# Layer-0 attention: the reciprocals of the softmax sums go through scratch memory by DMA, not through TensorE transposes

## The chip, the cores and the metric

The kernel runs on one core of a Trainium2 chip. The metric is the device time of one execution, in microseconds (us); a smaller time is better. The engines are TensorE (PE; its weight loads are listed as PEld), VectorE (DVE), ScalarE (ACT), GpSimd (POOL) and SyncE (SP), and SP's queue issues nearly all DMAs.

## What is computed

Four layers of a diffusion trunk on 512 latent tokens and 256 context tokens of width 1024: grouped-query attention, neighbourhood attention, a convolution module and a Fourier mixer, each followed by an MLP. The change is in layer 0, whose mixer is this (16 query heads, 4 key heads, head size 64; `ctx_out` is true there, so the context's own attention is computed too):

```python
def gqa_attend(q, k, v):
    s = jnp.einsum('bqkgd,bnkd->bkgqn', q, k, preferred_element_type=jnp.float32)
    p = jax.nn.softmax(s, axis=-1).astype(v.dtype)
    return jnp.einsum('bkgqn,bnkd->bqkgd', p, v)
...
    ob = lax.map(lambda q: gqa_attend(q, k_all, v_all), qb)
    yl = ob.transpose(1, 0, 2, 3, 4, 5).reshape(B, S, AT_WIDTH) @ w_o
...
        oc = gqa_attend(qc.reshape(B, C, AT_KV_HEADS, AT_GROUP, HEAD_DIM), kc, vc)
        yc = oc.reshape(B, C, AT_WIDTH) @ w_o
```

The softmax's division is not made on the probabilities. The kernel multiplies exp(s) with the values first, and the product with 1/sum afterwards.

## The kernel before

Layer 0's attention is `l0b`. Its work is 8 pairs of heads (`pair`) x 3 parts of 256 query tokens (`part`: 0 and 1 are latent tokens with all 768 keys, 2 is the context with its 256 keys) x 2 heads (`hh`). A group is one (pair, part), so there are 24 groups. Below, (p,1) is part 1 of pair p.

For each item, `front` runs twice (`u`), for 128 tokens each time. It makes the scores (L612, PE into `ps_s`), their negated maximum (L614, DVE), the exponentials `p` with their sums in `sums` (L616, ACT), transposes of `p` (L621, PE into `ps_st`), and the split of these into a high and a low part `pt` (L104 on ACT, L105 on DVE). `back`, one item later, multiplies with the values (L635, PE into `ps_pv`, which is one buffer).

When both heads of a group are through, `recip_rows` turns the sums round. Sums lie with tokens on partitions, and the product lies with tokens along the free axis. The reciprocal is taken on DVE (L555), spread to 64 columns a head on DVE (L557, `tmp_q`), transposed twice on PE (L559, into a `ps_st` buffer, of which there are three) and copied out by ACT (L561, `tmp_r`, called `rb` in the code). `fold` adds the two halves of the product (L567 on ACT, L568 on DVE, twice each a group, into `tmp_t`). `scale_pv` multiplies `tmp_t` with `rb` on POOL (L573), and splits the result into `o` (the cast L104 on ACT, the subtraction L105 on POOL).

SP's queue in this stage holds the stores of the last `qd` rows (L530), a load of 768 KB of `q` for each pair (L586), six loads of output weights (`raw`, L113), and at the end `sb`, the four loads of `x` (L667) and the `araw` tiles for the projection with `wo0` that follows.

The order on each engine's queue is not the code's. A scheduler sets it at build time by its own estimates (L1338), and the engines then run their queues strictly in that order: an instruction that waits holds all that stand behind it on its engine.

Of the kernel before, what the change touches and what calls it, by code (L numbers as in the profile page):

```python
# [9 lines left out]
F = mybir.dt.float32  # L10
# [6 lines left out]
P = 128  # L17
# [7 lines left out]
HD = 64  # L25
# [24 lines left out]
class Trunk:  # L50
# [499 lines left out]
    def recip_rows(self, sums, w, wk, rp):  # L550
# [10 lines left out]
        nc.scalar.copy(out=rb, in_=rp[:, :w])  # L561
        return rb

    def fold(self, pv, hh, t):

        a, b = slice(hh * HD, hh * HD + HD), slice(HD - hh * HD, 2 * HD - hh * HD)
        self.nc.scalar.copy(out=t[a], in_=pv[b])  # L567
        self.nc.vector.tensor_tensor(out=t[a], in0=pv[a], in1=t[a], op=ALU.add)  # L568
# [7 lines left out]
    def l0b(self):  # L576
        nc, io = self.nc, self.io
# [3 lines left out]
        wk = self.open("att0", "right")  # L581
# [7 lines left out]
        def keys(part):  # L589
            return (0, 6) if part < 2 else (4, 2)  # L590
# [34 lines left out]
        def back(pair, part, hh, half):  # L625

            k0, nk = keys(part)
            if hh == half == 0:
                pvs[pair, part] = self.ps("pv")
            sums, pv = groups[pair, part], pvs[pair, part]  # L630
            pt = heads[pair, part, hh]
            o_ = pv[:, hh * 256:hh * 256 + 256]
            for c in range(k0 + half * nk // 2, k0 + (half + 1) * nk // 2):
                for s in range(2):
                    nc.tensor.matmul(o_, self.vp[:, c, pair // 2].rearrange("p s d -> p (s d)"), pt[s][:, :, c - k0],  # L635
                                     start=(hh == s == 0 and c == k0), stop=(hh == s == 1 and c == 5))
            if hh == half == 1:
                t0 = part * 256
                rb = self.recip_rows(sums, 256, wk, self.ps("st"))
                t = self.tmp("t", 256)  # L640
                for e in range(2):
                    self.fold(pv[:, e * 256:e * 256 + 256], e, t)
                self.scale_pv(t, rb, (o[pair][:, 0, t0:t0 + 256], o[pair][:, 1, t0:t0 + 256]))
# [4 lines left out]
        for i in range(len(work) + 1):  # L648
            if i < len(work) and work[i][1:] == (0, 0) and work[i][0] < 7:
                load(work[i][0] + 1)  # L650
            for u in range(2):
                if i < len(work):
                    front(*work[i], u)
                if i > 0:
                    back(*work[i - 1], u)
            if i == LATE:
                self.late()
                self.open("att0b", "right")
# [699 lines left out]
```

## Time and profile before

| what | us |
|---|---|
| median of 3 runs | 2750.66 |
| lowest and highest run | 2748.48 and 2753.79 |
| the profiled execution, its own time | 2748.76 |
| its span in the trace | 2747.0 |
| layer-0 attention, from the first reciprocal to the last fold | 191.8 to 386.4 |
| one pair of heads in the steady part of it | 23.7 |

The profile is of one execution. A row gives busy time and idle time of instructions, and the idle time is put down to the instruction that came last. In the layer-0 attention three engines are busy at once, so a share of busy time alone does not name the one that sets the pace; waits between them must be read with it.

### The profile page before, as it was taken

Reading aid. Unit: us, or ns where it says so; the run is one execution under the profiler, and the core shown is the slowest. Engines: PE = TensorE matmul, PEld = TensorE weight load, DVE = VectorE, ACT = ScalarE, POOL = GpSimd, SP = SyncE. Lnnn points to the kernel's source line nnn. Section 1 sums busy time; section 2 is a strip of 40 time slices with the busy share of each in tenths; the row PEclk is TensorE's granted clock in tenths of the full one; section 3 lists DMA queues with packets and bytes.
Section 4 is the critical chain, followed back from the end, with each engine's and each line's share of the span. In section 5 each row is a group of like instructions: output and inputs, shape, how many; then the busy total and the mean of one; then the engine's idle time right before and its main releaser. Section 6 shows DMA issues by size and latency. Waiting matters only on the chain.

```text
span 2747.0 us, 39895 instructions
## 1 busy us (share of the span) xinstructions
PE 2638.0 (96%) x15472; PEld 2316.5 (84%) x15472; DVE 1776.1 (65%) x2827; ACT 1154.8 (42%) x2052; POOL 405.4 (15%) x359
## 2 busy tenths in 40 slices
PE   7989899999999999998999999998999998999998
PEld 5878778888888888988988889888888887988888
DVE  7988879766453372268766657998666657644445
ACT  3458864212121342268523335656322245533323
POOL 2321212000000030034200004543000012200002
PEclk8999999999999999999999999999999999999999
DMA  7431234445442256488466644213466633333334
GB/s 269 133 123 36 77 120 147 139 145 153 137 140 85 77 168 209 138 201 190 161 206 207 190 147 139 77 47 107 133 212 200 206 124 107 123 115 94 98 100 123
DMA packets 124844, 384.85 MB, mean 140 GB/s; under 512 B 17264, under 2 KB 37872, under 8 KB 123632
## 3 DMA queue, kind: packets, MB, share of 16 engines
q1 hardware_dynamic: 121392, 379.17, 44.2%
q10 hardware_dynamic: 3264, 3.15, 0.3%
q8 instruction: 122, 2.00, 0.3%
q14 instruction: 66, 0.54, 0.1%
HBM read 354.98 MB, written 27.26 MB: 139 GB/s over the span
## 4 chain that ended last, share of the span: by engine, by line
PE 49%; DVE 4%; DMA 2%; ACT 1%; issue 0%; POOL 0%; DVEq 0%; SPq 0%; ACTq 0%; POOLq 0%
PE ps_mm L124 15%; PE ps_mm L125 15%; PE ps_mm L127 15%; DVE ps_st L1162 1%; DMA k<-k 1%; DMA q<-q 1%; PE ps_cv L124 1%; PE ps_cv L125 1%; PE ps_cv L127 1%; DVE h L182 0%; PE ps_s L881 0%; PE ps_pt L890 0%; PE ps_cv L995 0%; PE ps_cv L998 0%; PE ps_cv L999 0%
## 5 line engine op out<-in xcount | busy, mean ns | idle before, releaser
L104 ACT CAST wh<-raw 128x1024 fp32r<-128x1024 f32 (+1 forms) x397 | 419.6, 1060 | 1030.6 <-PE ps_mm L125 606.5
L105 DVE TENSOR_TENSOR wl<-raw,wh 128x1024 fp32r<-128x1024 f32 (+1 forms) x368 | 463.7, 1262 | 372.6 <-ACT wh L104 369.5
L194 POOL TENSOR_TENSOR S<-S,tmp_q 128x256 f32<-128x256 f32 (+1 forms) x104 | 144.8, 1392 | 1684.8 <-ACT tmp_q L193 1680.7
L124 PE MATMUL ps_mm<-u,wh 128*128 128x512 f32 (+1 forms) x1088 | 374.9, 346 | 0.0
L125 PE MATMUL ps_mm<-u,wh 128*128 128x512 f32 (+1 forms) x1088 | 373.8, 345 | 0.0
L127 PE MATMUL ps_mm<-u,wl 128*128 128x512 f32 (+1 forms) x1088 | 373.6, 346 | 0.0
L125 PE MATMUL ps_mm<-hm,wh 128*128 128x512 f32 (+1 forms) x912 | 331.2, 365 | 0.0
L127 PE MATMUL ps_mm<-hm,wl 128*128 128x512 f32 (+1 forms) x912 | 331.0, 365 | 0.0
L124 PE MATMUL ps_mm<-hm,wh 128*128 128x512 f32 (+1 forms) x912 | 328.2, 366 | 1.1 <-ACT hm L181 1.1
L223 DVE CUSTOM_DVE_ANT_0 prod<-araw,sb 128x1024 bf16<-128x1024 f32 x224 | 276.4, 1234 | 6.5 <-DMA araw<-in_ada 5.3
L206 DVE SCALAR_TENSOR_TENSOR x<-ps_mm,mod,x 128x256 f32<-128x256 f32 (+1 forms) x192 | 115.1, 605 | 246.8 <-PE ps_mm L127 241.1
L125 PEld LDWEIGHTS ps_mm<-u,wh 128*128 128x128 f32 x1088 | 206.1, 189 | 25.0
L127 PEld LDWEIGHTS ps_mm<-u,wl 128*128 128x128 f32 x1088 | 205.9, 189 | 25.2
L124 PEld LDWEIGHTS ps_mm<-u,wh 128*128 128x128 f32 x1088 | 205.7, 189 | 25.3 <-DVE x L206 0.4
L127 PEld LDWEIGHTS ps_mm<-hm,wl 128*128 128x128 f32 x912 | 172.6, 189 | 27.6 <-DVE wl L105 0.4
L125 PEld LDWEIGHTS ps_mm<-hm,wh 128*128 128x128 f32 x912 | 172.7, 190 | 27.2
L124 PEld LDWEIGHTS ps_mm<-hm,wh 128*128 128x128 f32 x912 | 170.8, 190 | 28.7 <-ACT hm L181 1.5
L104 ACT CAST u<-tmp_r 128x512 fp32r<-128x512 f32 (+2 forms) x143 | 89.0, 624 | 171.1 <-DVE tmp_r L738 170.9
L124 PE MATMUL ps_big<-hm,wh 128*128 128x512 f32 x464 | 157.4, 339 | 0.8 <-ACT wh L104 0.8
L105 DVE TENSOR_TENSOR u<-tmp_r,u 128x512 fp32r<-128x512 f32 (+2 forms) x143 | 99.1, 695 | 86.6 <-ACT u L104 86.2
L125 PE MATMUL ps_big<-hm,wh 128*128 128x512 f32 x464 | 145.9, 337 | 0.0
L124 PE MATMUL ps_mm<-wh,h 128*128 128x256 f32 x448 | 129.9, 291 | 7.3 <-DVE tmp_r L499 2.9
(311 smaller groups left out, 5781.6 us busy)
## 6 DMA issues: line engine op xcount, KB each, us to landing
raw<-in_w SPq DMA_DIRECT2D x288, 512.0 KB, 3.9
araw<-in_ada SPq DMA_DIRECT2D x176, 512.0 KB, 3.7
raw<-in_wo SPq DMA_DIRECT2D x32, 512.0 KB, 4.3
raw<-in_wpw SPq DMA_DIRECT2D x24, 512.0 KB, 3.5
raw<-in_wqk SPq DMA_DIRECT2D x16, 512.0 KB, 4.1
q<-q SPq DMA_DIRECT2D x32, 256.0 KB, 9.1
raw<-in_wft SPq DMA_DIRECT2D x16, 512.0 KB, 3.8
k<-k SPq DMA_DIRECT2D x32, 224.0 KB, 9.4
```

The costliest lines, as they stand in the source:

```text
L104: self.nc.scalar.copy(out=H, in_=src)
L105: (low or self.nc.vector).tensor_tensor(out=L, in0=src, in1=H.bitcast(F), op=ALU.subtract)
L124: mm(o, lhs[0], rh, start=(k == 0), stop=False)
L125: mm(o, lhs[0], rl, start=False, stop=False)
L127: mm(o, lhs[1], rh, start=False, stop=last)
L194: (add or nc.gpsimd).tensor_tensor(out=S[:, :w], in0=S[:, :w], in1=q, op=ALU.add)
L206: self.nc.vector.scalar_tensor_tensor(out=xm, in0=self.like(ps), scalar=gate[:, m:m + 1], in1=xm, op0=ALU.mult, op1=ALU.add)
L223: ins = self.nc.vector.tensor_tensor_reduce(out=junk, in0=t, in1=self.sb[:, v], op0=ALU.mult, op1=ALU.add, scale=1.0, scalar=0.0, accum_ou ...
L1162: keep(nc.vector.scalar_tensor_tensor(out=y if last else a, in0=ut, scalar=wt, in1=a, op0=ALU.mult, op1=ALU.add))
```

## The change

`back` calls a new function, `recip_spread`, instead of `recip_rows`. The reciprocal on DVE stays. The spreading copy (DVE), the two transposes (PE), their `ps_st` buffer and the copy out of it (ACT) are gone. In their place SP issues two stores that write the reciprocals of one head each, transposed, to a scratch row in DRAM (`rrow`), element by element of 4 bytes from 128 partitions, and two loads that read a head's row of 256 floats back to 64 partitions each (`tmp_r`). A load needs the stores to have landed. `recip_rows` is still used by layer 1.

```diff
+    def recip_spread(self, sums, wk):
+
+        nc = self.nc
+        rs = wk.tile([P, 2, 2], F, tag="rs", name="rs", bufs=3)
+        nc.vector.reciprocal(out=rs, in_=sums)
+        row = self.dram.tile([2, 2, P], F, tag="rrow", name="rrow", bufs=3)
+        rb = self.tmp("r", 256)
+        for hh in range(2):
+            nc.sync.dma_start(row[hh].rearrange("b p -> p b"), rs[:, :, hh])
+        for hh in range(2):
+            nc.sync.dma_start(rb[hh * HD:hh * HD + HD], row[hh].rearrange("b p -> (b p)").unsqueeze(0).to_broadcast([HD, 256]))
+        return rb
...
-                rb = self.recip_rows(sums, 256, wk, self.ps("st"))
+                rb = self.recip_spread(sums, wk)
```

The scheduler lays all queues anew. In the changed kernel lines behind L563 are 13 higher (L616 is L629, L586 is L599).

SP's queue before, from the last `qd` stores to the first loads for the projection:

```order
L530 DMA qd<-qs 256x1x256 x12
L586 DMA q<-qd 128x1536 x6
L113 DMA raw<-in_wo 128x1024 x6
L282 DMA sb<-sdram 128x2048
L667 DMA x<-in_xT 128x1536 x4
```

SP's queue now, in the steady part, from part 0 of one pair to part 0 of the next (`rrow<-rs` is the two stores of a group, `tmp_r<-rrow` its two loads, `q<-qd` the load for the pair after next):

```order
L572 DMA rrow<-rs 128x2x1 x2
L574 DMA tmp_r<-rrow 64x256 x2
L572 DMA rrow<-rs 128x2x1 x2
L574 DMA tmp_r<-rrow 64x256 x2
L599 DMA q<-qd 128x1536
L572 DMA rrow<-rs 128x2x1 x2
L574 DMA tmp_r<-rrow 64x256 x2
L572 DMA rrow<-rs 128x2x1 x2
L574 DMA tmp_r<-rrow 64x256 x2
```

Four transfers a group have come into SP's queue; the load of `q` stands between part 1's and part 2's, and at the end of the stage the last group's four stand ahead of `sb` and `x`.

ACT's queue before, in pair 3, from the cast of part 1's result into `o` (first row) to that of part 2's (last row):

```order
L104 CAST o_3_1947<-tmp_t 128x256
L104 CAST pt_3381<-ps_st 128x384
L567 COPY tmp_t<-ps_pv 64x256
L616 ACTIVATE p,sums<-ps_s,small_m 128x768
L104 CAST pt_3381<-ps_st 128x384 x2
L567 COPY tmp_t<-ps_pv 64x256
L561 COPY tmp_r<-ps_st 128x256
L616 ACTIVATE p,sums<-ps_s,small_m 128x768
L104 CAST pt_3446<-ps_st 128x384 x2
L616 ACTIVATE p,sums<-ps_s,small_m 128x768
L104 CAST pt_3446<-ps_st 128x384
L104 CAST o_3_1947<-tmp_t 128x256
```

The same stretch of ACT's queue now:

```order
L104 CAST o_3_1947<-tmp_t 128x256
L580 COPY tmp_t<-ps_pv 64x256
L629 ACTIVATE p,sums<-ps_s,small_m 128x768
L104 CAST pt_3370<-ps_st 128x384 x2
L580 COPY tmp_t<-ps_pv 64x256
L104 CAST pt_3434<-ps_st 128x384
L629 ACTIVATE p,sums<-ps_s,small_m 128x768
L104 CAST pt_3434<-ps_st 128x384 x2
L104 CAST o_3_1947<-tmp_t 128x256
```

The copy of `tmp_r` is gone, and part 2's cast stands one exponential (128x768) and one cast of `pt` earlier. Part 1's cast has kept the same work between it and the sums that it depends on, less one copy of `tmp_r`.

## Rows read from the trace of the kernel before

**Rows 1.** The page: busy time of each engine, its share, instructions.

```profile
PE 2638.0 (96%) x15472; PEld 2316.5 (84%) x15472; DVE 1776.1 (65%) x2827; ACT 1154.8 (42%) x2052; POOL 405.4 (15%) x359
```

**Rows 2.** Windows: from:to length, busy (instructions) by engine, PEclk, DMA share, GB/s.

```profile
243.51:267.19 23.68, 21.84 (x161) 19.34 (x160) 21.40 (x44) 21.06 (x58) 4.44 (x6) 1.00 0.10 34
...
335.00:340.00 5.00, 2.16 (x10) 1.30 (x10) 3.67 (x6) 4.93 (x11) 4.66 (x3) 0.86 0.35 105
340.00:345.00 5.00, 5.00 (x22) 4.81 (x23) 4.37 (x9) 4.03 (x10) 1.47 (x2) 0.50 0.65 210
...
400.00:420.00 20.00, 18.49 (x79) 14.41 (x79) 19.77 (x26) 5.49 (x8) 4.43 (x3) 1.00 0.55 178
```

**Rows 3.** Groups of instructions, 243.51 to 267.19 (pair 2): busy us, mean ns | idle before.

```profile
L621 PE MATMUL ps_st<-ident,p 128*128 128x128 f32 x59 | 9.8, 277 | 1.8 <-ACT p L616 1.1 <-ACT tmp_r L561 0.6
L104 ACT CAST pt<-ps_st 128x384 fp32r<-128x384 f32 x18 | 8.3, 489 | 1.2 <-PE ps_st L621 1.2
L616 ACT ACTIVATE p<-ps_s,small_m 128x768 f32<-128x768 f32 x8 | 7.3, 912 | 0.0
L573 POOL TENSOR_TENSOR tmp_t<-tmp_t,tmp_r 128x256 f32<-128x256 f32 x3 | 2.2, 740 | 16.4 <-DVE tmp_t L568 12.5 <-ACT pt L104 3.9
L567 ACT COPY tmp_t<-ps_pv 64x256 f32<-64x256 f32 x6 | 2.2, 368 | 1.2 <-PE ps_pv L635 1.0
L559 PE MATMUL ps_st<-ident,tmp_q 128*128 128x128 f32 x6 | 1.1, 272 | 0.0
L561 ACT COPY tmp_r<-ps_st 128x256 f32<-128x256 f32 x3 | 1.1, 375 | 0.1
L557 DVE COPY tmp_q<-rs 128x256 f32<-128x256 f32 x3 | 0.9, 287 | 0.0
```

**Rows 4.** Timeline of pair 2: start, duration, instruction; reciprocals, POOL's products, casts of `o`.

```profile
252.81 0.17 DVE L555 RECIPROCAL rs<-sums 128x4 f32<-128x4 f32 x1
256.89 0.18 DVE L555 RECIPROCAL rs<-sums 128x4 f32<-128x4 f32 x1
...
260.91 0.74 POOL L573 TENSOR_TENSOR tmp_t<-tmp_t,tmp_r 128x256 f32<-128x256 f32 x1 [6.33 <-DVE tmp_t L568]
...
262.18 0.43 ACT L104 CAST o<-tmp_t 128x256 fp32r<-128x256 f32 x1
...
268.71 0.45 ACT L104 CAST o<-tmp_t 128x256 fp32r<-128x256 f32 x1
```

**Rows 5.** DMA issues on the whole span: count, KB each, median us from issue to landing.

```profile
q<-qd SPq DMA_DIRECT2D x8, 768.0 KB, 4.3
...
qd<-qs SPq DMA_DIRECT2D x12, 256.0 KB, 2.5
...
k<-ks SPq DMA_DIRECT2D x16, 64.0 KB, 4.3
...
z<-nz SPq DMA_DIRECT2D x4, 4.0 KB, 1.7
```

**Rows 6.** What SP's queue takes to issue them: ns minimum/median/maximum, first and last start.

```profile
L530 SPq DMA_DIRECT2D qd<-qs x12: 512/513/902, 164.4 to 200.2; - x12
...
L586 SPq DMA_DIRECT2D q<-qd x8: 320/324/428, 143.5 to 326.4; - x8
```

**Rows 7.** Timeline at the stage's end: last reciprocal and product, SP's loads, `x`.

```profile
380.35 0.18 DVE L555 RECIPROCAL rs<-sums 128x4 f32<-128x4 f32 x1
...
386.47 0.73 POOL L573 TENSOR_TENSOR tmp_t<-tmp_t,tmp_r 128x256 f32<-128x256 f32 x1 [1.12 <-DVE tmp_t L568]
...
383.99 0.33 SPq L282 DMA_DIRECT2D sb<-sdram  x1
384.37 2.98 SPq L667 DMA_DIRECT2D x<-in_xT  x4
...
391.88 0.75 DVE L206 SCALAR_TENSOR_TENSOR x<-ps_mm,mod,x 128x512 f32<-128x512 f32 x1 [5.50 <-DMA x<-in_xT]
```

## Prediction

> **What bounds the kernel now.** I read the page first. PE is busy for 96% of the span [rows 1], so over the whole kernel work taken off PE should come off the time. But the change touches one stage, so I read that stage next. In the steady part of the layer-0 attention a pair of heads takes 23.68 us, and in it PE is busy for 21.84, DVE for 21.40 and ACT for 21.06 [rows 2]. No engine is the bound alone: each is idle for some 2 us of the pair, and the idle time of each is put down to another of them. PE's transposes of `p` wait 1.1 us for ACT's exponentials and 0.6 us for ACT's copy into `tmp_r`, which has to free a `ps_st` buffer, and ACT's casts of `pt` wait 1.2 us for these transposes [rows 3]. It is a ring of PE and ACT with DVE close behind. POOL is idle for most of the pair, and what its product waits for is the second fold on DVE in 12.5 us of its idle time [rows 3], not the reciprocals. So the reciprocals' way to the other layout ends early today, and a slower way has room. How much room is the question of this case.
>
> **What is removed.** A pair has three groups. PE loses six transposes, 1.1 us a pair, and with them the wait of 0.6 us for `tmp_r` [rows 3]; if PE alone set the pace that would be 1.7 us a pair. ACT loses three copies of 375 ns, 1.1 us a pair. DVE loses three copies of 287 ns, 0.9 us a pair [rows 3]. The reciprocal stays. As the three engines wait for each other, the pair can't shrink by less than the least of these unless something new waits, and by little more than the greatest, so the bounds are 0.9 and 1.7 us. I take 1.2 us, close to ACT's, since ACT ends most of PE's waits. Over eight pairs that is 9.6 us, with 7 and 14 as ends.
>
> **What is added: the way of one group.** SP issues two stores, waits for both to land, and issues two loads. No store of 4-byte elements is in this trace. Nearest is the `qd` store, which is also written out of SBUF by SP with a three-dimensional pattern: 0.51 us to issue [rows 6], 2.5 us to land [rows 5]. From below stands the 4 KB store `z<-nz` with 1.7, from above the 64 KB store `k<-ks` with 4.3 [rows 5]. It stands behind larger ones on the same queue, so its own time is less. I take 2.5. A load is issued in 0.32 us, as `q` [rows 6]; it moves 64 KB, between the 1.7 us of 4 KB and the 2.5 us of 256 KB [rows 5], so I take 2.2 to land. The way is 2 x 0.51 + 2.5 + 2 x 0.32 + 2.2 = 6.4 us from the reciprocal to `rb`, with 4.8 and 10.3 as ends, if I let both transfers take 1.7 or both 4.3.
>
> **What covers it.** The place that matters is ACT's queue: the cast of `o` waits for POOL's product, and behind it in ACT's queue stand the exponentials and the casts of `pt` that PE and DVE live on. So `rb` has to be there one product (0.74 us) ahead of the cast. The order of the changed kernel tells what stands between.
>
> Part 1: the reciprocal at 252.81, the cast at 262.18 [rows 4], 9.37 us apart. Now the same work stands between, less one `tmp_r` copy of 0.375. So 9.37 - 0.375 - 0.74 = 8.25 us are left for 6.4.
>
> Part 2: 256.89 to 268.71 is 11.82 us [rows 4]. Now one exponential (0.91), one cast of `pt` (0.49) and two `tmp_r` copies (0.75) stand no longer between [rows 3], so 11.82 - 2.15 - 0.74 = 8.9 us are left. But part 2's way is longer, since SP's queue is in order. Its reciprocal comes 4.08 us after part 1's [rows 4], and SP is free for it 2 x 0.51 + 2.5 + 2 x 0.32 + 0.32 = 4.5 us after part 1's, for part 1's loads and the load of `q` stand ahead: 0.4 us late. The stores then share the queue with the 768 KB of `q`, which land 4.3 us after their issue [rows 5], so the stores land some 3.8 us after the first one's issue has ended rather than 2.5. The way is 0.4 + 1.03 + 3.8 + 0.65 + 2.2 = 8.1 of 8.9 us. It is the tightest place, with 0.8 us to spare.
>
> Part 0 has nothing ahead of it in SP's queue, and its cast of `o` has moved later, not earlier. It is covered. I put the steady part's added cost at nothing. The load of `q` itself is for the pair after next, a whole pair of 23.7 us ahead, and being 1 or 2 us later costs nothing.
>
> **The ends of the stage.** The first group's loads stand ahead of the last four `qd` stores in SP's queue; ACT's `qs` buffers wait for these. I put 0.3 us. At the end SP has to see the last group's stores landed before it can issue `sb` and `x`: 380.35 + 0.18 + 1.03 + 2.5 + 0.65 = 384.7 instead of 383.99 [rows 7], 0.7 us late. DVE waits 5.50 us for `x` there [rows 7], and after it the projection runs with DVE at 19.77 of 20 us [rows 2], so a later `x` is a later end: 0.6 us, with 0 and 2 as ends. The last product on POOL is at 386.47, 6.1 us after its reciprocal [rows 7], against a way of 6.4; the context's part of the projection needs it much later, so that is nothing. The scheduler also moved rows in later stages, whose counts on PE, DVE and ACT are the same. I see no sign in it and give it nothing, with 2 us to each side.
>
> **The sum.** -9.6 + 0.3 + 0.6 = -8.7 us: the profiled execution's 2748.76 would be 2740.1, and the median 2750.66, which lies 1.9 us above it, would be 2742.0.
>
> **Rivals.**
>
> *The small stores are slow, and the kernel is slower.* The mechanism: the stores hold SP's in-order queue until they land, part 2's way grows by 2 us for each us of their landing time (it starts later and lasts longer), its cast of `o` stops ACT, and with ACT the ring. With s for the landing time, part 2's way is (s - 2.1) + 1.03 + max(s, 3.8) + 2.85. It passes 8.9 at s = 3.3. From s = 4.1 on the stall of some 1.1 us a pair eats the 8.7 us. At s = 4.3, the row of `k<-ks` [rows 5], it is 10.4, or 1.5 us a pair: 12 us lost, 3.5 slower, 2754. At s = 5.5 part 1 falls out too (9.4 of 8.25) and part 2 needs 12.8: 1.1 + 3.9 = 5 us a pair, 40 lost, 2782. For it: the stores write 4 bytes at a time, and no row shows such a thing. Against it: `k<-ks` carries 32 times the bytes behind other stores. The Trainium skill speaks against this change (DMA: Bandwidth & Descriptors, section Rules for kernel authors): a strided last dimension lowers to one descriptor per element, and a transpose should not be made by a plain DMA with a rearranged access pattern. By that rule a store here has 256 descriptors, as many as the `k<-ks` store has runs, and the sum would go by 4.3 rather than 2.5, and come out at +3.5 rather than -8.7. No row tells whether the count or the bytes decide. I give this rival 0.18.
>
> *The gain is not had.* The ring may be held by what was not touched (exponential, transposes of `p`, casts), so that the freed time turns into other waits, or part 2's cast stalls a little (s = 3.6 gives 0.3 us a pair, 2.4 in all). Half of 9.6 gives 2750.66 - 4.8 + 0.9 = 2746.8. For it: PE's wait for exponentials (1.1) is greater than its wait for `tmp_r` (0.6) [rows 3]. Against it: all three engines shed work. I give 0.27.
>
> *The clock.* From 335 to 340 PE was busy for only 2.16 of 5 us, while ACT and POOL split the first `wo0` weights, and in the next 5 us the granted clock is 0.50, the lower of the two levels (1.2 GHz) [rows 2]. In the changed kernel these casts stand at other places. If PE doesn't pause there, some 2.5 us more are won; if it pauses once more elsewhere, 2.5 are lost. It changes no sign, and is within the range.
>
> That the change does not do what it says can be left out: the 48 transposes are gone from PE's queue in the order.
>
> **How the numbers follow.** This measurement can tell some 0.2% (5.5 us) from no change. The forecast (2742, from 2736 to 2745) has 0.55, the gain not had (2745 to 2751) 0.27, the slow stores (2751 and up) 0.18. From 2736 to 2755 leaves out the far part of the slow case and a gain above 14 us, together 0.2. Faster by over 0.2% 0.56, within 0.2% 0.27, slower 0.17.
>
> **What would show it.** Right: pairs of 22.5 us instead of 23.7; PE's wait for `tmp_r` gone; POOL's product still waiting for the second fold; the stores landing in under 3.3 us; `x` issued under 1 us later against the last reciprocal. Wrong: ACT's cast of `o` waiting for POOL, and POOL for a DMA, above all in part 2; pairs of 23.7 us with other waits in the place of `tmp_r`'s; `x` some us late.

## The result, and the profile after

The changed kernel takes 2870.17 us (median of 4 runs, 2864.61 to 2872.8) against 2749.57 in the same comparison: a ratio of 1.0437, with an interval of 1.0425 to 1.0449. It is 121 us slower. The prediction of 2742 was wrong in sign, and the time lies far above its range.

The page of the changed kernel, busy times first, then the chain of work that ended last, by engine and by line:

```profile
PE 2659.6 (93%) x15424; PEld 2338.0 (82%) x15424; DVE 1772.6 (62%) x2803; ACT 1153.4 (40%) x2028; POOL 405.0 (14%) x359
...
PE 76%; DMA 9%; DVE 9%; ACT 3%; issue 2%; SPq 1%; POOL 0%; DVEq 0%; POOLq 0%; ACTq 0%
PE ps_mm L124 17%; PE ps_mm L125 17%; PE ps_mm L127 17%; PE ps_big L124 6%; PE ps_big L127 6%; PE ps_big L125 6%; DMA rrow<-rs 4%; DVE prod L223 2%; DMA k<-k 2%; DMA tmp_r<-rrow 1%; PE ps_st L634 1%; PE ps_pv L648 1%; DVE wl L105 1%; DVE h L182 1%; PE ps_s L625 1%
```

PE has 48 instructions less than in [rows 1], and its share fell from 96% to 93%: PE waits. On the chain stands `rrow<-rs`, the small store, with 4% of the span (3.7% before rounding, some 106 us). The place is the layer-0 attention. A window of the changed kernel there, from one load of `q` to the next (columns as in [rows 2]):

```profile
298.86:340.90 42.04, 22.59 (x150) 20.57 (x149) 20.88 (x41) 20.89 (x53) 4.37 (x6) 0.80 0.17 29
```

This stretch takes 42.04 us instead of 23.68, all three engines are idle for about half of it, and the granted clock fell from 1.00 to 0.80 with PE's pauses. It is among the longest: by the last reciprocals of the pairs, the seven pairs after the first take 34 to 43 us, 37.5 on the mean, against 24.4 before. What the engines waited for, in the stage (us in total, times, longest):

```profile
POOL tmp_t L586 <- DMA tmp_r<-rrow: 157.1, 15, 15.3
PEld ps_st L634 <- ACT p L629: 92.7, 23, 11.2
ACT o L104 <- POOL tmp_t L586: 87.5, 15, 11.7
PE ps_st L634 <- ACT p L629: 87.4, 23, 11.0
DVE pt L105 <- ACT pt L104: 52.4, 29, 11.5
```

Read from the top, this is a chain: POOL's product waits for the loads, ACT's cast of `o` for POOL, and PE's transposes and DVE for the exponentials and casts that stand behind that cast in ACT's queue. In [rows 3] POOL's product waited for DVE's fold, and no DMA was in sight. The transfers themselves (count, KB each, median us from issue to landing):

```profile
q<-qd SPq DMA_DIRECT2D x8, 768.0 KB, 6.1
...
tmp_r<-rrow SPq DMA_DIRECT2D x48, 64.0 KB, 3.8
...
rrow<-rs SPq DMA_DIRECT2D x48, 1.0 KB, 8.5
```

A store of 1 KB takes 8.5 us to land, twice what 64 KB took in [rows 5]. Other transfers land later too: `q` went from 4.3 to 6.1. One group's way in the timeline of the changed kernel, with the reciprocal of part 2 first:

```profile
292.47 0.18 DVE L568 RECIPROCAL rs<-sums 128x4 f32<-128x4 f32 x1 [0.36 <-ACT p L629]
...
289.04 1.90 SPq L572 DMA_DIRECT2D rrow<-rs  x2
297.05 1.77 SPq L574 DMA_DIRECT2D tmp_r<-rrow  x2
298.86 0.59 SPq L599 DMA_DIRECT2D q<-qd  x1
299.49 1.41 SPq L572 DMA_DIRECT2D rrow<-rs  x2
...
309.79 1.09 SPq L574 DMA_DIRECT2D tmp_r<-rrow  x2
310.92 1.10 SPq L572 DMA_DIRECT2D rrow<-rs  x2
...
320.41 0.72 POOL L586 TENSOR_TENSOR tmp_t<-tmp_t,tmp_r 128x256 f32<-128x256 f32 x1 [15.31 <-DMA tmp_r<-rrow]
...
321.17 0.40 ACT L104 CAST o<-tmp_t 128x256 fp32r<-128x256 f32 x1 [11.68 <-POOL tmp_t L586]
```

SP is held from 290.94 to 297.05 by part 1's stores, so part 2's stores go out at 299.49, 7.0 us after their reciprocal. They land only by 309.79. The loads issued then have next to them the following group's stores (310.92), and POOL's product starts at 320.41. From reciprocal to cast it is 28.7 us where [rows 4] had 11.8.

The first loads behind the stage tell where the rest is. `sb`, issued at the end of the attention, comes 114.1 us later than in [rows 7] (498.05), and the end of the program 121.4 later. So the stage costs 114, and the later stages, whose work is the same, another 7. By the reciprocals of part 2, the 114 are 9 in the first pair, 91 in the seven others (13.0 each), and 13 between the last reciprocal and `sb`.

### The profile page after: what moved, and what is told of

Same layout as the page of the kernel before. It is cut to its first block, busy times and chain, and to the rows that moved or that the text cites. A ratio compares the mean times of both kernels' runs of the same rounds, so it can differ in the third digit from the quotient of the medians.

```text
span 2868.4 us, 40039 instructions
## 1 busy us (share of the span) xinstructions
PE 2659.6 (93%) x15424; PEld 2338.0 (82%) x15424; DVE 1772.6 (62%) x2803; ACT 1153.4 (40%) x2028; POOL 405.0 (14%) x359
## 4 chain that ended last, share of the span: by engine, by line
PE 76%; DMA 9%; DVE 9%; ACT 3%; issue 2%; SPq 1%; POOL 0%; DVEq 0%; POOLq 0%; ACTq 0%
PE ps_mm L124 17%; PE ps_mm L125 17%; PE ps_mm L127 17%; PE ps_big L124 6%; PE ps_big L127 6%; PE ps_big L125 6%; DMA rrow<-rs 4%; DVE prod L223 2%; DMA k<-k 2%; DMA tmp_r<-rrow 1%; PE ps_st L634 1%; PE ps_pv L648 1%; DVE wl L105 1%; DVE h L182 1%; PE ps_s L625 1%
## 5 line engine op out<-in xcount | busy, mean ns | idle before, releaser
L124 PEld LDWEIGHTS ps_mm<-hm,wh 128*128 128x128 f32 x912 | 170.8, 190 | 28.7 <-ACT hm L181 1.5
L634 PE MATMUL ps_st<-ident,p 128*128 128x128 f32 x448 | 84.0, 313 | 104.5 <-ACT p L629 89.4
L124 PE MATMUL ps_big<-hm,wh 128*128 128x512 f32 x464 | 157.4, 339 | 0.8 <-ACT wh L104 0.8
L634 PEld LDWEIGHTS ps_st<-ident,p 128*128 128x128 f32 x448 | 59.2, 160 | 113.3 <-ACT p L629 95.0
```

Source lines behind the costliest of these rows:

```text
L124: mm(o, lhs[0], rh, start=(k == 0), stop=False)
L634: nc.tensor.transpose(pp[:, i * P:(i + 1) * P], p[:, (c + i) * P:(c + i + 1) * P], self.ident)
```

## The experiments

My theory after the result: the store is slow because its 4-byte pieces lie next to each other in memory. The rivals: the number of pieces (256 a store), the wait between store and load whatever the store, SP's queue, and the scheduler's new order, which most versions of the change share but for a few places.

**No wait for the stores.** The stores stay as they are; the loads read a row that was written at the start, so the products are meaningless.

```diff
+        flat = self.orow.rearrange("p b h -> (p b h)")
-            nc.sync.dma_start(rb[...], row[hh]...)
+            nc.sync.dma_start(rb[...], flat[hh * 256:hh * 256 + 256].unsqueeze(0).to_broadcast([HD, 256]))
```

> The changed kernel with its stores as they are, but the loads read a row of ones that was written once at the start, so no load waits for a store (the output is not divided by the sums). Theory A (what costs is the wait for the stores to land, on SP's in-order queue and on the way of each group): the stores still take 7 to 9 us to land and the time is within 5 us of the run without any way, 2740 to 2746 us. Rival B (the small stores clog the DMA rings, so that the loads behind them land late whether or not they wait): loads land after 6 us or more, POOL still waits for them, 2780 us or more.

Measured: 2790.11, ratio 1.0154 (1.0137 to 1.0172). Two thirds of the loss go with the wait, but not all. No load waits for a store here, and still 41 us are lost: `sb` is issued 23 us late, and 19 us come behind it. Neither case of the expectation holds as it stands. The time is above that of theory A and within rival B's, but POOL isn't seen to wait for the loads as B had it. This trace has no landing times.

**Pieces of 16 bytes.** One store a group, 128 pieces of 16 bytes, contiguous; the loads wait for it. The row's elements stand in another order than the product needs.

```diff
-        row = self.dram.tile([2, 2, P], F, tag="rrow", name="rrow", bufs=3)
+        row = self.dram.tile([P, 2, 2], F, tag="rrow", name="rrow", bufs=3)
+        nc.sync.dma_start(row, rs)
```

> The changed kernel with one store a group that writes the same bytes untransposed: 128 runs of 16 bytes instead of 512 of 4 bytes. The loads read 256 floats each as before and wait for the store (the values stand in the wrong places). Theory A (the number of pieces sets the landing time): the store lands in 2.5 to 4 us instead of 8.5, the way is 0.5 + 3 + 0.9 + 3.8 = 8 us, near its cover, and the time is 2740 to 2770 us. Rival B (a write to scratch memory in pieces far under 512 bytes, or a load right behind a store, is slow whatever their number): the store still takes 7 us or more, and the time is above 2830 us.

Measured: 2760.6, ratio 1.0044 (1.003 to 1.0058). Its transfers:

```profile
tmp_r<-rrow SPq DMA_DIRECT2D x48, 64.0 KB, 2.7
...
rrow<-rs SPq DMA_DIRECT2D x24, 2.0 KB, 2.3
```

With a store that lands in 2.3 us the round trip through memory is covered, as the prediction had it for 2.5. POOL waits 1.4 us in all for a DMA. So the wait between store and load is not what costs; the landing time is. The queues have the order of the changed kernel but for two places, so 110 of the 121 us hang on the form of the store alone.

**The same number of pieces, 512 bytes apart**, with the loads from the old row as in the first run.

```diff
-        row = self.dram.tile([2, 2, P], F, tag="rrow", name="rrow", bufs=3)
+        row = self.dram.tile([2, 2, P, P], F, tag="rrow", name="rrow", bufs=3)
-            nc.sync.dma_start(row[hh].rearrange("b p -> p b"), rs[:, :, hh])
+            nc.sync.dma_start(row[hh].rearrange("b p n -> p b n")[:, :, 0:1], rs[:, :, hh:hh + 1])
```

> As the run whose loads read an old row, with the same order of all queues, but the stores write their 4-byte elements 512 bytes apart instead of side by side (the output is not divided by the sums). Theory A (the number of pieces sets the landing time, wherever they go): stores land after 7 to 9 us as before. Rival B (the pieces of several DMA engines meet in the same few hundred bytes of memory and wait for each other there): stores land in 4 us or less. The time of the kernel should be the same as that run's within 5 us, since nothing waits for the stores.

Measured: 2772.15 (one run).

```profile
tmp_r<-orow SPq DMA_DIRECT2D x48, 64.0 KB, 2.6
...
rrow<-rs SPq DMA_DIRECT2D x48, 1.0 KB, 1.9
```

256 pieces of 4 bytes land in 1.9 us when they are far apart. The count is out. The program has the instruction order of the first run and is 18 us faster, where the expectation had the same time within 5 us, though in neither does a load wait for a store. 17 of the 18 us are there when `sb` is issued. The three steady pairs between the loads of `q` take 71.1 us in both runs; the difference comes where ACT waits for other transfers. These waits of the first run are absent here:

```profile
205.19 0.59 ACT L533 CAST qs<-ps_st 128x512 fp32r<-128x512 f32 x1 [5.49 <-DMA qd<-qs]
...
351.57 1.04 ACT L104 CAST wh<-raw 128x1024 fp32r<-128x1024 f32 x1 [6.25 <-DMA raw<-in_wo]
...
359.69 1.04 ACT L104 CAST wh<-raw 128x1024 fp32r<-128x1024 f32 x1 [4.60 <-DMA raw<-in_wo]
```

So adjacent pieces hold up other transfers, and it costs time where an engine waits for one of those.

**The distance, from 4 to 512 bytes, doubled from pair to pair.** The loads read the old row.

```diff
+        d = 1 << n // 3
+        row = self.dram.tile([2, 2, P, d], F, tag=f"rrow{d}", name=f"rrow{d}", bufs=3)
```

> The stores of the changed kernel with the elements 4 bytes apart in pair 0, 8 in pair 1, then 16, 32, 64, 128, 256 and 512 bytes apart in pair 7; the loads read a row that was written at the start, so no one waits for a store and the products are meaningless. The count of pieces (256 a store) is the same in all pairs. If the count decides, all land alike. If the distance decides, the landing falls from about 8 us at 4 bytes to about 2 at 512; a fall in proportion to the distance would mean that pieces in one block of memory are written one after the other, a step at one distance that the block has that size. The whole is 2772 to 2785.

Measured: 2769.11 (one run), a little under the range. The store's landing in this run, one line for each pair, from 4 bytes in the first to 512 in the last (us, minimum/median/maximum; the large maxima are of stores behind the 768 KB of `q`; not every landing is recorded):

```profile
DMA to landing us min/median/max: 7.6/9.2/10.7
...
DMA to landing us min/median/max: 3.0/4.2/8.7
...
DMA to landing us min/median/max: 2.5/2.5/2.6
...
DMA to landing us min/median/max: 1.8/3.6/3.7
...
DMA to landing us min/median/max: 1.5/2.3/5.2
...
DMA to landing us min/median/max: 1.5/1.6/1.8
...
DMA to landing us min/median/max: 1.5/1.6/1.6
...
DMA to landing us min/median/max: 1.5/1.7/3.5
```

The minima are 7.6, 3.0, 2.5, 1.8 us at 4, 8, 16 and 32 bytes, and 1.5 from 64 bytes on. The time falls with the distance and is flat from 64 on, neither in proportion to the distance nor in one step. So the distance decides, but neither of the readings that the expectation gave to such a fall is shown, and why near pieces are slow stays open.

**The loads issued by POOL**, so that SP no longer stands still between a store and its load. POOL does, in its place.

```diff
-            nc.sync.dma_start(rb[hh * HD:hh * HD + HD], ...)
+            nc.gpsimd.dma_start(rb[hh * HD:hh * HD + HD], ...)
```

> The changed kernel with the two loads of a group issued by POOL and not by SP, so that SP issues stores (and q) without a wait between. Theory: in the changed kernel SP spends 10.5 us a group on store, wait and load, one group after the other, 31 us for the three groups of a pair; with SP free, only the landing time of one group (8.5 plus about 4 us) counts against its cover of some 8 us, so the pairs take 28 to 32 us instead of 42 and the whole is 2780 to 2820. Rival: it is the latency of each group alone that stops POOL's product and ACT's cast, and SP's queue adds nothing; the pairs stay near 42 and the whole near 2870. Second rival: POOL, which now waits itself for the stores before it issues, is held longer, and it is slower than 2870.

Measured: 2849.77 (one run), above the theory's 2820, below the rival's 2870. The waits in the stage:

```profile
POOL tmp_r L574 <- DMA rrow<-rs: 131.3, 21, 17.5
...
POOL tmp_t L586 <- DMA tmp_r<-rrow: 48.4, 8, 8.4
```

Of the 121 us, 20 go when SP isn't held by the stores. The store's own time (8.1 us here) stays, and POOL waits for it. The scheduler's order changed with the edit as well, so the 20 us are not SP's queue alone.

**No way at all.** No stores, no loads; POOL multiplies with constants.

```diff
-        row = self.dram.tile([2, 2, P], F, tag="rrow", name="rrow", bufs=3)
-        rb = self.tmp("r", 256)
...
-        return rb
+        return self.vecs[:, :256]
```

> The changed kernel with the way taken out: the reciprocal on DVE stays, there are no stores and no loads, and POOL multiplies with 256 columns of the constant tile vecs, so the products in layer 0 are meaningless. What is left is the bare removal of 6 transposes, 3 copies on ACT and 3 on DVE a pair. If the prediction's gain of 1.2 us a pair is there, the pairs take 22.5 us and the whole 2740 to 2743. If the ring is held by work that was not touched (the kernel with distant elements, where no one waits for a store, had pairs of 23.1 to 24.9 us), the pairs stay near 23.7 and the time is 2745 to 2752. If the scheduler's new order of the later stages costs time by itself (by the kernel with distant elements some 17 us), the stage ends early and the whole is still at 2755 to 2765.

Measured: 2757.42, ratio 1.0027 (1.0014 to 1.004). By its time this is the third case of the expectation, though the stage doesn't end early as that had it. The removal with nothing in its place, in the order that the scheduler then lays, makes the kernel slower. The steady pair, and PE's transposes of `p` in it:

```profile
258.48:282.60 24.12, 20.64 (x155) 18.71 (x154) 20.84 (x42) 20.63 (x54) 4.44 (x7) 1.00 0.10 33
```

```profile
L628 PE MATMUL ps_st<-ident,p 128*128 128x128 f32 x56 | 8.8, 276 | 3.3 <-ACT p L623 1.8 <-DVE pt L105 1.4
```

PE is busy 1.2 us less a pair than in [rows 2], and its transposes of `p` wait 1.5 us more than in [rows 3]. The wait for `tmp_r` is gone; those for the exponentials and for DVE's half of `pt`, which frees the `ps_st` buffers, have grown past it. `sb` is issued 2.0 us late, the final stores 9.0, so 7 of the 9 us come in later stages, whose work has not changed but whose order has.

**The same in the old order.** Every queue from the attention to the end is tied, by issue-order edges without waits, to the order that it had in the kernel before, less the removed rows. `OLD` holds that order as a table of numbers.

```diff
+    def hold(self, traced):
+        for e, (n, code) in OLD.items():
...
+            for a, b in zip(row, row[1:]):
+                self.tc.add_manual_dep(b, a.name, info, reason="old order")
```

> The way taken out as in the run without a way (no stores, no loads, POOL multiplies with 256 columns of the constant tile vecs, the products of layer 0 are meaningless), but now every queue from the layer-0 attention to the end keeps the order of the kernel before, less the removed rows (6 transposes, 3 copies on ACT and 3 on DVE a pair). The run without a way took 2757 with the scheduler's new order, pairs of 24.1 us and PE waiting for exponentials. If the new order is what ate the gain, the pairs now take 22.3 to 22.8 us and the whole 2737 to 2742, as the prediction had it for the removal. If the ring can't go faster whatever the order, because the exponentials, the transposes of p and the casts hold one another, the pairs stay at 23.3 to 23.7 and the whole at 2745 to 2750.

Measured: 2748.49, ratio 0.9999 (0.9989 to 1.0008). A pair, and PE's transposes:

```profile
254.16:277.21 23.05, 20.75 (x154) 18.69 (x154) 20.67 (x43) 20.32 (x55) 4.43 (x7) 1.00 0.09 35
```

```profile
L654 PE MATMUL ps_st<-ident,p 128*128 128x128 f32 x56 | 9.1, 274 | 1.7 <-ACT p L649 1.0 <-DVE pt L118 0.7
```

The result lies between the two expectations: the pair gains 0.63 us, less than the theory's 0.9 at the least, more than the rival's 0.4, and the whole is as the rival had it. PE waits 1.7 us a pair where it waited 1.8 in [rows 3]. The 0.6 us on `tmp_r` became 0.7 on `pt`.

**A way with longer pieces, in the scheduler's order.** The whole computation: DVE takes the reciprocals into 32 columns and turns them in blocks of 32 x 32, one store writes 128-byte pieces, four loads read them.

```diff
+        nc.vector.transpose(re[:, 32:], re[:, :32])
+        nc.sync.dma_start(row.rearrange("k c j -> (k c) j"), re[:, 32:])
```

> The whole computation with the scratch row written in longer pieces: DVE takes the reciprocals into 32 columns (eight times the same four), turns them in blocks of 32 x 32, and one store a group writes 128 pieces of 128 bytes next to each other; four loads a group read them back. Theory (short pieces next to each other make the landing slow): the store lands in 2 to 3 us as the store of 16-byte pieces did (2.3), no one waits for a DMA, the pairs take 24 to 25 us, and the whole is 2752 to 2768, near the 2760 of the kernel with 16-byte pieces. Rival (any store and load round trip through scratch memory of this kind is slow): landing 7 us or more and 2850.

Measured: 2773.56, ratio 1.0087 (1.0065 to 1.0109), some 5 us above the range. The store lands in 1.7 us, as expected, but POOL still waits 73.9 us for the four loads of 32 KB (3.4 us to land, one behind the other in SP's queue). In this order DVE's turn also stands up to 2.4 us behind the end of the reciprocal.

**The same, two loads, in the old order.** The store lays the four rows that are read contiguous, so that two loads a group do, and DVE's turn is tied right behind the reciprocal.

```diff
-        row = self.dram.tile([4, 32, 32], F, tag="rrow", name="rrow", bufs=3)
+        row = self.dram.tile([32, 4, 32], F, tag="rrow", name="rrow", bufs=3)
+        nc.sync.dma_start(row.rearrange("c k j -> k c j"), re[:, 32:])
...
+            nc.sync.dma_start(rb[...], row[2 * hh:2 * hh + 2].rearrange("c k j -> (c k j)").unsqueeze(0).to_broadcast([HD, 256]))
```

> The whole computation, in the order of the kernel before. DVE takes the reciprocals into 32 columns and turns them in blocks of 32 x 32 right behind, one store a group writes pieces of 128 bytes (the four rows that are read lie contiguous), two loads a group read 1 KB rows back. Theory (short adjacent pieces made the store slow, and the order ate the gain): landing 1.5 to 2.5 us, no wait of POOL for a DMA in the steady part, pairs of 22.5 to 23.2 us (DVE has 0.2 us a group more than without a way), and the whole 2740 to 2748, at or under the kernel before. Rival: the round trip of about 6 us is still too long for the casts of part 2, POOL waits for the loads, and the whole is 2755 to 2775 like the kernel with the turn on DVE in the scheduler's order (2774).

Measured: 2751.83, ratio 1.0012 (1.0001 to 1.0024), a few us above the theory's range and under the rival's. POOL's products wait for the fold again, as in [rows 4]:

```profile
260.90 0.74 POOL L614 TENSOR_TENSOR tmp_t<-tmp_t,tmp_r 128x256 f32<-128x256 f32 x1 [6.28 <-DVE tmp_t L609]
```

```profile
252.97:276.19 23.22, 20.89 (x155) 18.70 (x154) 21.76 (x45) 20.22 (x55) 4.43 (x7) 1.00 0.17 54
```

This is the change as it was meant, with its faults mended: the way is hidden, the pair is 0.46 us shorter, and the kernel is no faster. Which of the three mends (two loads, the turn's place, the order) did most was not separated. None of the versions beats the kernel before.

**The changed kernel in the old order.** Only the order is held; the stores stay.

```diff
+        k.hold(nc.cur_bb.bb.instructions[k.n0:])
```

> The changed kernel, stores of 4-byte elements next to each other, with all queues in the order of the kernel before (less the removed rows; the new transfers where the scheduler puts them). Theory: SP's queue with 1.0 + 8.5 + 0.65 us and the landing of the loads for each group still sets the pace, three groups in 31 us or more, so the pairs take 36 to 42 us and the whole is 2830 to 2870. Rival: the order was a main part of the loss, and the whole is under 2810.

Measured: 2842.11 (one run), as the theory had it; the pairs take 33 to 38 us, some of them under the theory's 36. Its span is 2840.3, against 2746.9 without the way and 2868.4 in the scheduler's order. So the 121 us divide into 0 for the removal, 93 for the way with adjacent 4-byte stores, and 28 for the order that the scheduler chose for it (20 in the stage, by the issue of `sb`, and 8 later). The last two rest on one run of this kernel, and they hold for this way of taking the change apart: without a way the scheduler's order costs 9 us, not 28.

## Why the prediction was wrong, point by point

**What is removed (9.6 us): wrong, nearly nothing.** Two things failed. The durations of single instructions were added up, but instructions on one engine overlap. In the kernel before, the exponential starts 0.27 us after a copy of `tmp_r` that is listed with 0.38:

```profile
258.72 0.38 ACT L561 COPY tmp_r<-ps_st 128x256 f32<-128x256 f32 x1
258.99 0.91 ACT L616 ACTIVATE p<-ps_s,small_m 128x768 f32<-128x768 f32 x1
```

With the order held, busy time fell by 1.09 (PE), 0.73 (DVE) and 0.74 us (ACT) a pair against [rows 2], where the sum had 1.1, 0.9 and 1.1. And the lower bound of 0.9 "unless something new waits" was taken as safe. Something did: PE's wait for a `ps_st` buffer passed from `tmp_r` to `pt`, and 0.63 us a pair were left. From the first reciprocal to the issue of `sb` the stage became 2.9 us shorter, and in the whole kernel nothing of it can be measured. The rival *the gain is not had* named this (the wait for the exponentials greater than that for `tmp_r`) and put it at half; it was more.

**The store's landing (2.5 us): wrong, and this decided.** The value was that of `qd<-qs`, with 4.3 from `k<-ks` as the upper end [rows 5], on the ground that 1 KB must take less than 64 KB. Measured: 8.5, and never under 7.1. Both ends were rows with pieces of a size and a distance unlike this store's, so the range was bounded on the wrong scale: bytes, where the distance of the pieces counts. The lower end, 1.7 from `z<-nz`, was misread besides: that transfer goes from one tile in SBUF to another, not to DRAM. And `k<-ks` writes 256 pieces too (of 256 bytes) and took 4.3, so the number of pieces would not have told it either. With this term the steady part's added cost, put at nothing, became the greatest of all: the seven pairs after the first grew by 91 us.

**The load's landing (2.2) and its issue (0.32): too low.** 3.8 and 0.45, up to 10.0 beside the stores. With quick stores it was 2.6 to 2.7.

**The cover: right in its mechanism.** 8.25 and 8.9 us were given for a way of 6.4 and 8.1. With a store of 2.3 us POOL waits 1.4 us in the whole stage; with the turned rows in the old order its products wait for the fold. It is tight, as the prediction had it: with a store of 1.7 us but four loads, in the scheduler's order, POOL waits 73.9 us.

**Rival one, slow stores: the right mechanism, with too small a size and chance.** SP held, part 2 late, its cast stopping ACT, and ACT the ring: the waits show each link. Its own formula at s = 8.5 gives 8.5 - 2.1 + 1.03 + 8.5 + 2.85 = 18.8 for part 2 and 12.4 for part 1, so 9.9 + 4.2 = 14 us a pair, 112 less 8.7: some 103 us slower, near the stage's 114. That it comes so near is in part luck: the formula has 2.2 us for a load that took up to 10.0, and knows nothing of the 28 us that went with the order. The price was followed only up to s = 5.5, and the chance was 0.18.

By the Trainium skill (DMA: Bandwidth & Descriptors, section Rules for kernel authors) the store has one descriptor for each element, and a transpose isn't made this way. The runs bear out the advice but not a price by the count: 256 pieces land in 8.5 us next to each other and in 1.9 us 512 bytes apart. The measurement decides.

**The ends (+0.3, +0.6): both too low.** At the start, ACT waits 7.6 us for one `qd` store, which stands behind the first group's loads in SP's queue; in the kernel before, all ACT's waits for such stores were 8.9 us together. From the last reciprocal to `sb` it was to be some 4.4 us:

```profile
480.97 0.18 DVE L568 RECIPROCAL rs<-sums 128x4 f32<-128x4 f32 x1 [0.36 <-ACT p L629]
...
486.39 1.10 SPq L572 DMA_DIRECT2D rrow<-rs  x2
496.85 1.09 SPq L574 DMA_DIRECT2D tmp_r<-rrow  x2
498.05 0.52 SPq L282 DMA_DIRECT2D sb<-sdram  x1
...
505.44 0.75 DVE L206 SCALAR_TENSOR_TENSOR x<-ps_mm,mod,x 128x512 f32<-128x512 f32 x1 [12.60 <-DMA x<-in_xT]
```

It is 17.1, and DVE's wait for `x` is 12.60 us where it was 5.50 [rows 7].

**Later stages (0, 2 us to each side): too narrow.** In the scheduler's orders the later stages lost 2 to 19 us: 7 in the changed kernel and without a way, 18 in the run with distant pieces. Not all of that is the order, for the three runs that read the old row have one order and lost 19, 18 and 11 there. Where the old order was held, it was 3 us or less.

**The clock (2.5 us to either side): too small.** The granted clock is 0.80 in the stretch shown of the changed kernel, where PE pauses, and 1.00 in the pair without a way. It follows from the waits and adds to them: PE's busy time is 21.6 us greater than in [rows 1] with 48 instructions less. How much of the 121 us that makes was not separated.

## What to carry to other kernels

Before small rows are sent through memory, look at how far apart the pieces of the store lie, not at its bytes: write pieces of 16 bytes or more, or turn the block first. Work taken off a ring of engines that wait for each other is worth what the next wait leaves of it; take the removed work out with nothing in its place, and with the order held, before pricing what replaces it. Where a scheduler lays the queues, an edit in one stage can move the others by several us, and a prediction's range has to hold that.

## What the runs showed of the hardware

- A store of 256 pieces of 4 bytes lands in 7.6 us at the quickest when they are adjacent (7.1 in the changed kernel), 3.0 at a distance of 8 bytes, 2.5 at 16, 1.8 at 32, and 1.5 from 64 bytes on, in the run with the distances.
- Adjacent stores delay other transfers that are not ordered behind them: in the changed kernel `q` landed in 6.1 us and loads of `tmp_r` in 3.8 (10.0 at most), with distant pieces in 4.9 and 2.6 (3.9 at most). With no load waiting for a store, the stage was 17 us longer with adjacent pieces than with distant ones.
- A round trip through DRAM, one store of 128 pieces of 128 bytes and two loads of 64 KB behind it, fits into the 7.9 us from a reciprocal (252.97) to its product (260.90) in the run with the turned rows and the old order; the store of the same size in the scheduler's order landed in 1.7.
